# Sparse heads' value products: high and low half of the values in one stationary operand, joined by a permutation product

## The chip, the cores and the metric

One Trainium2 chip, one of its cores. The metric is the device time of one execution in microseconds (us). The cores' engines are named as in the profile: PE is TensorE (matmuls; PEld its weight loads), DVE is VectorE, ACT is ScalarE, POOL is GpSimd, SP issues most of the DMAs.

## What is computed

Two transformer layers on 512 tokens of width 1024. Each layer has eight sliding-window heads (kind "a"), eight sparse heads (kind "b") that share one key and value head and attend to the 128 best keys of an indexer, an output projection with layer norm, then a gated feed-forward part with a second layer norm. The sparse heads' part, cut to what matters here:

```python
_, sel = lax.top_k(idx_score, k_top)
ks = gather(k, sel)
vs = gather(v, sel)
s = jnp.einsum('bqhgd,bqjhd->bqhgj', qb, ks) * (D ** -0.5)
s = jnp.where(valid[:, :, None, None, :], s, NEG)
pr = jax.nn.softmax(s, axis=-1)
o = jnp.einsum('bqhgj,bqjhd->bqhgd', pr, vs)
```

The kernel gathers nothing: it adds a mask of 0 or -1e30 to the scores of all earlier keys, so that `o` is a product of a masked softmax with all values. The heads are 64 wide.

## The kernel before

The tokens stand in four tiles `t` of 128. All matmuls outside the window heads' value products work in the type fp32r, which is coarser than fp32; to keep the accuracy a number is held as a high part (rounded to fp32r) and a low part (the rest), and a product of two such pairs is three matmuls: high by high, high by low, low by high. That is `mm3` (lines 314 to 318).

Attention works in units (kind, `t`, `g`): a group `g` of four heads for one tile of queries, `units` in line 734: first the eight of kind "a", then the eight of kind "b" with `t` rising. `scores` (lines 638 to 673) makes a unit's scores on PE (L656), adds the mask and takes the maximum on DVE (L660), and takes the exponentials and their sums on ACT (L664). `values` (lines 675 to 732) follows two units later. For every block `b` of 128 keys it turns the four heads' probabilities on PE (L698); for kind "b" ACT casts the turned block out of the PSUM bank as the high part (L701) and DVE subtracts to get the low part (L702). Then `pv(b)`, `LAG` = 2 blocks later for kind "b", multiplies with the values. A unit of tile `t` has `t` + 1 blocks, so a layer's eight sparse units have 2 x (1 + 2 + 3 + 4) = 20 blocks.

The result of a unit has to hold two heads on 128 partitions (64 each). So the values stand in a tile `vb[t]` with zeros beside them, the high part in columns 64 to 127 and the low part in 192 to 255 (lines 563 to 576), and `pv` takes for the even head (`u` = 0) a window [values, zeros] and for the odd head [zeros, values]; both add up in the same 256 columns of one bank. With three matmuls for each of the two windows that is six matmuls of 256 columns to a block. At the end of the unit DVE multiplies the bank by the reciprocal sums (L723), ACT casts the product (L730) and POOL takes the low part (L731); they go into `fh` and `fl`, from where the second half of the output projection, `last_o` (lines 820 to 825), reads them.

What sets the order of the instructions: the streams of a layer are Python generators that `Order.run` takes turns with by the costs that they yield; `order.later(delay, fn)` puts off a piece of work until the running cost has grown by `delay` (`tick`). So the program is written with the two halves of the projections, the scores, the values and the top-k mixed. Then the tile framework orders each engine's instructions once more by a simulated timeline. On the chip every engine works its list off in that order. All PSUM tiles come from one pool of eight banks of 512 fp32 columns. While the sparse units run, PE also has the output projection's first half (`rest`, lines 804 to 812, "wsp,slot" in the rows) to do; the second half (`last_o`, 96 matmuls, "wsp,fh") comes when the attention is through, but the scheduler lets it begin under the last unit's products. After `last_o` each tile's sum goes through the first layer norm (`ln_sums`, lines 395 to 404), is turned by PE (`to_features`, lines 406 to 415) and feeds the first `gate_up`.

The weights are split by ACT (L269, high part) and POOL (L270, low part) as soon as one of five buffers `wsp` comes free.

Of the kernel before, what the change touches and what calls it, by code (L numbers as in the profile page):

```python
# [34 lines left out]
NSLOT, NTMP = 28, 12  # L35
D_GI, D_K, D_Q, AHEAD = 9.0, 8.0, 10.0, 2
IDX_PACE, NSTART, R_MAIN, R_TOP = 1.5, 2, 0.75, 0.001
# [4 lines left out]
class Order:  # L42
# [10 lines left out]

    def later(self, delay, fn):
        self.held.append((self.now + delay, fn))

# [31 lines left out]
def hybrid_kernel(ctx: ExitStack, tc: tile.TileContext, x, p, positions, ln_in_g, ln_in_b, w_in,  # L88
# [234 lines left out]
    V.tensor_scalar(idf, jp, 0.0, None, op0=OP.is_equal)  # L323
    V.tensor_copy(idr, idf)
    causal = const.tile([128, S], F32, name="causal")
    G.memset(causal[:, :S - 128], 0.0)
# [184 lines left out]
    for l in range(L):  # L511
# [47 lines left out]
        def kv_out(t, ps):  # L559
# [3 lines left out]
            vb[t] = slot()  # L563
            G.memset(vb[t][:, :320].bitcast(F32), 0.0)
            kss = []
            for c0, n, o in ((0, 2, 0), (2, 1, 256)):
# [3 lines left out]
                for i in range(n):  # L570
                    v = o + (n + i) * 64
                    if c0 + i < 2:
                        A.copy(vt[t][:, 64 + 128 * (c0 + i):128 * (c0 + i + 1)], ps[:, v:v + 64])
                    else:
                        A.copy(vb[t][:, 64:128], ps[:, v:v + 64])
                        V.tensor_tensor(vb[t][:, 192:256], ps[:, v:v + 64], vb[t][:, 64:128], OP.subtract)
                kss.append((c0, n, ks))
# [97 lines left out]
        def values(kind, t, g, st):  # L675

            es, rb, b0, nb = st
            c = g if kind == "a" else 2
            o = acc()[:, :256].rearrange("p (a n) -> p a n", a=2)
            pts = {}  # L680
            lag, cost = LAG[kind], (0.65 if kind == "b" else 0.87)
            if kind == "b":
                yield from wait("x read")

            def pv(b):
                for u in range(2):
                    if kind == "b":
                        h, lo = vb[b0 + b][:, 64 - 64 * u:192 - 64 * u], vb[b0 + b][:, 192 - 64 * u:320 - 64 * u]
                        mm3(o, h, lo, pts[b][0][:, u], pts[b][1][:, u], b == 0 and u == 0, b == nb - 1 and u == 1)
                        continue  # L690
                    f = 64 + 128 * c - 64 * u
                    PE.matmul(o, vt[b0 + b][:, f:f + 128], pts[b][:, u], start=b == 0 and u == 0,  # L692
                              stop=b == nb - 1 and u == 1)
# [26 lines left out]
            for b in range(max(0, nb - lag), nb):  # L720
                pv(b)
                yield cost
            V.tensor_tensor(of, o, rr, OP.mult)  # L723
            if kind == "a":
# [318 lines left out]
```

## Time and profile before

| | before |
|---|---|
| median of 3 runs | 1281.9 us (1280.48 to 1283.91) |
| the profiled execution's own time | 1279.94 us |
| its span, first to last instruction | 1277.8 us |
| PE busy | 1240.9 us, 97% of the span |
| PE weight loads | 1072.5 us, 84% |
| DVE, ACT, POOL busy | 807.2, 569.9, 710.5 us |
| mean granted TensorE clock | 0.988 of full speed |
| DMA | 112.77 MB, mean 88 GB/s |

The busy time of PE counts a matmul from its start to an end that is modelled, and matmuls overlap in the array; so a busy PE is read by the distance from one matmul's start to the next. A row of the timeline gives the start, the duration, the engine and line, the operation with the tiles it writes and reads, and in brackets the idle time before it with what ended that. The wait of an instruction is put down to what came last.

### The profile page before, as it was taken

The numbers are of one execution on the slowest core, as the hardware profiler recorded it, in microseconds if no ns is written. First come the engines' busy times: TensorE is split into PE (matmuls) and PEld (weight loads), VectorE is DVE, ScalarE is ACT, GpSimd is POOL, SyncE is SP. The second block draws the span as 40 slices with busy tenths as digits, with TensorE's granted clock in tenths as the row PEclk, the third lists the DMA queues.
The fourth block names the chain that finished last, engine by engine and source line by source line (L and its number), as shares of the span: only waits on it lengthen the run. The fifth ranks groups of instructions, "written<-read, shape, count | busy, mean of one in ns | idle before, by whom it ended". The sixth has DMA issues, their size and how long they took to land.

```text
span 1277.8 us, 18295 instructions
## 1 busy us (share of the span) xinstructions
PE 1240.9 (97%) x6632; PEld 1072.5 (84%) x6632; DVE 807.2 (63%) x1762; ACT 569.9 (45%) x1192; POOL 710.5 (56%) x589
## 2 busy tenths in 40 slices
PE   6899999899999999999999999999999999999996
PEld 4799889788888888888898998979888888888885
DVE  7799855864545454545679996675736363645376
ACT  2567765344333433334336677743434342434320
POOL 7777532357474757573068855234656575747422
PEclk9899999999999999999998999999999999999998
DMA  5133221333232324134023313104242423231321
GB/s 173 51 98 101 66 68 34 99 115 92 91 112 86 117 81 131 34 100 142 12 68 104 111 34 117 49 20 135 93 133 67 132 74 124 83 99 38 111 83 50
DMA packets 89122, 112.77 MB, mean 88 GB/s; under 512 B 5444, under 2 KB 65860, under 8 KB 89032
## 3 DMA queue, kind: packets, MB, share of 16 engines
q1 hardware_dynamic: 88360, 111.58, 28.2%
q8 instruction: 52, 0.85, 0.3%
q14 instruction: 38, 0.31, 0.1%
q10 hardware_dynamic: 672, 0.03, 0.0%
HBM read 109.49 MB, written 2.10 MB: 87 GB/s over the span
## 4 chain that ended last, share of the span: by engine, by line
PE 83%; DVE 7%; POOL 4%; issue 2%; DMA 2%; ACT 1%; SPq 0%; DVEq 0%; POOLq 0%; ACTq 0%
PE bank L316 25%; PE bank L317 25%; PE bank L318 25%; PE bank L656 3%; PE bank L698 2%; POOL wsp L270 2%; PE bank L692 2%; POOL wsp L248 1%; DMA wst<-in_w_pg_dram 1%; PE bank L486 1%; DVE work L620 1%; DVE x L404 1%; PE bank L412 1%; PE bank L715 1%; DVE fl L415 1%
## 5 line engine op out<-in xcount | busy, mean ns | idle before, releaser
L270 POOL TENSOR_TENSOR wsp<-wst,wsp 128x1024 fp32r<-128x1024 f32 (+2 forms) x148 | 353.3, 2400 | 270.8 <-ACT wsp L269 265.9
L317 PE MATMUL bank<-fl,wsp 128*128 128x512 f32 (+1 forms) x768 | 285.7, 373 | 2.0 <-DVE fl L415 2.0
L316 PE MATMUL bank<-fh,wsp 128*128 128x512 f32 (+1 forms) x768 | 284.2, 373 | 1.0 <-ACT fh L414 1.0
L318 PE MATMUL bank<-fh,wsp 128*128 128x512 f32 (+1 forms) x768 | 283.9, 372 | 0.0
L269 ACT CAST wsp<-wst 128x1024 fp32r<-128x1024 f32 (+2 forms) x148 | 151.2, 1032 | 167.6 <-PE bank L318 115.7
L841 DVE TENSOR_TENSOR t2k<-bank,t2k 128x512 f32<-128x512 f32 x44 | 30.4, 692 | 221.8 <-PE bank L318 221.8
L317 PEld LDWEIGHTS bank<-fl,wsp 128*128 128x128 f32 x768 | 145.5, 189 | 27.5 <-DVE fl L415 2.4
L316 PE MATMUL bank<-wsp,fh 128*128 128x256 f32 (+3 forms) x512 | 165.8, 327 | 0.7 <-ACT fh L414 0.5
L318 PEld LDWEIGHTS bank<-fh,wsp 128*128 128x128 f32 x768 | 145.4, 189 | 25.1
L316 PEld LDWEIGHTS bank<-fh,wsp 128*128 128x128 f32 x768 | 144.2, 189 | 26.3 <-ACT fh L414 1.9
L318 PE MATMUL bank<-wsp,fl 128*128 128x256 f32 (+3 forms) x512 | 164.8, 323 | 1.1 <-DVE fl L415 1.1
L317 PE MATMUL bank<-wsp,fh 128*128 128x256 f32 (+3 forms) x512 | 165.5, 324 | 0.0
L248 POOL TENSOR_TENSOR wsp<-slot,wsp 128x512 fp32r<-128x512 f32 x100 | 141.2, 1438 | 29.5 <-ACT wsp L247 29.5
L316 PE MATMUL bank<-wsp,slot 128*128 128x512 f32 x392 | 153.7, 392 | 0.0
L317 PE MATMUL bank<-wsp,slot 128*128 128x512 f32 x392 | 152.7, 390 | 0.0
L318 PE MATMUL bank<-wsp,slot 128*128 128x512 f32 x392 | 148.5, 389 | 0.0
L773 DVE TENSOR_TENSOR x<-bank,x 128x512 f32<-128x512 f32 x140 | 91.5, 685 | 88.5 <-PE bank L318 88.5
L873 ACT CAST slot<-t2k 128x256 fp32r<-128x256 f32 (+1 forms) x104 | 49.8, 497 | 144.0 <-DVE t2k L841 102.5
L248 POOL TENSOR_TENSOR wsp<-t2k,wsp 128x512 fp32r<-128x512 f32 x40 | 57.5, 1449 | 92.2 <-ACT wsp L247 92.2
L316 PEld LDWEIGHTS bank<-wsp,fh 128*128 128x128 f32 x512 | 98.2, 192 | 7.6 <-ACT fh L414 1.4
L318 PEld LDWEIGHTS bank<-wsp,fl 128*128 128x128 f32 x512 | 98.0, 192 | 6.8 <-DVE fl L415 1.7
L317 PEld LDWEIGHTS bank<-wsp,fh 128*128 128x128 f32 x512 | 98.5, 192 | 5.8 <-POOL wsp L270 0.2
(166 smaller groups left out, 2186.6 us busy)
## 6 DMA issues: line engine op xcount, KB each, us to landing
wst<-in_w_gu_dram SPq DMA_DIRECT2D x88, 512.0 KB, 3.5
slot<-in_w_down_dram SPq DMA_DIRECT2D x80, 256.0 KB, 2.8
wst<-in_w_in_dram SPq DMA_DIRECT2D x16, 512.0 KB, 3.6
wst<-in_w_o_dram SPq DMA_DIRECT2D x16, 512.0 KB, 3.7
wst<-in_w_pg_dram SPq DMA_DIRECT2D x16, 512.0 KB, 4.4
wst<-in_w_in_dram SPq DMA_DIRECT2D x8, 256.0 KB, 2.7
lng<-in_ln_g_dram SPq DMA_DIRECT2D x4, 512.0 KB, 4.9
lnb<-in_ln_b_dram SPq DMA_DIRECT2D x4, 512.0 KB, 6.7
```

What stands on the lines that cost most here:

```text
L248: G.tensor_tensor(w[:, 1, j], src[j], w[:, 0, j], OP.subtract)
L269: A.copy(w[:, 0, :a * n], st[:, :a * n])
L270: G.tensor_tensor(w[:, 1, :a * n], st[:, :a * n], w[:, 0, :a * n], OP.subtract)
L316: PE.matmul(o, sh, mh, start=start, stop=False, skip_group_check=again)
L317: PE.matmul(o, sh, ml, start=False, stop=False, skip_group_check=again)
L318: PE.matmul(o, sl, mh, start=False, stop=stop, skip_group_check=again)
L656: PE.matmul(ps[:, o:o + nn], qT[kind, t, g][:, j * 128:(j + 1) * 128], kT[c, s][:, k0:k0 + nn], start=(s == 0), stop=(s == 1))
L692: PE.matmul(o, vt[b0 + b][:, f:f + 128], pts[b][:, u], start=b == 0 and u == 0, stop=b == nb - 1 and u == 1)
L698: PE.transpose(ps[:, j * 128:(j + 1) * 128], es[j][:, b * 128:(b + 1) * 128], idf)
L773: V.tensor_tensor(xt[t][:, c], ps, xt[t][:, c], OP.add)
L841: V.tensor_tensor(a, ps[1, f], a, OP.mult)
L873: A.copy(h[0], src)
```

## The change

The stationary operand of a sparse product now holds the values' high and low part side by side, so that no column of it is zero. `vb[t]` is [high, low, high] in three times 64 columns; the window from column 0 is [high, low] and the one from column 64 is [low, high]. A block takes two matmuls for each head, with the probabilities' high part and low part: four matmuls of 256 columns where there were six. The two heads go into two halves of the bank, 512 columns instead of 256: in the left half the partitions 0 to 63 hold what the high values gave for the even head, the partitions 64 to 127 what the low values gave, and in the right half it is the other way round for the odd head.

At the unit's end the halves have to be added across the partitions. ACT copies the whole bank into a tile `low` (type fp32r), and `merge`, put off by `D_LOW` = 1.5 and set at the head of the held list, multiplies it by a permutation `swap` that exchanges the upper and the lower 64 partitions, adding into the same bank: one matmul of 512 columns (line 745 of the changed file). After that DVE multiplies by the reciprocal sums in two instructions of 64 partitions, and ACT and POOL store as before (`store`). The zeroing of `vb` on POOL is gone; the high values are cast with a doubled output. The cost that a sparse product yields to the order is 0.48 instead of 0.65. `swap` is made once, on DVE, from the identity.

```diff
-D_GI, D_K, D_Q, AHEAD = 9.0, 8.0, 10.0, 2
+D_GI, D_K, D_Q, D_LOW, AHEAD = 9.0, 8.0, 10.0, 1.5, 2
...
-    def later(self, delay, fn):
-        self.held.append((self.now + delay, fn))
+    def later(self, delay, fn, soon=False):
+
+        self.held.insert(0 if soon else len(self.held), (self.now + delay, fn))
...
+    swap = const.tile([128, 128], F32R, name="swap")
+    V.tensor_copy(swap[:, :64], idf[:, 64:])
+    V.tensor_copy(swap[:, 64:], idf[:, :64])
...
             vb[t] = slot()
-            G.memset(vb[t][:, :320].bitcast(F32), 0.0)
...
-                        A.copy(vb[t][:, 64:128], ps[:, v:v + 64])
-                        V.tensor_tensor(vb[t][:, 192:256], ps[:, v:v + 64], vb[t][:, 64:128], OP.subtract)
+                        top = vb[t][:, :256].rearrange("p (u d) -> p u d", u=2)[:, :, :64]
+                        A.copy(top, ps[:, None, v:v + 64].to_broadcast([128, 2, 64]))
+                        V.tensor_tensor(vb[t][:, 64:128], ps[:, v:v + 64], vb[t][:, :64], OP.subtract)
...
-            o = acc()[:, :256].rearrange("p (a n) -> p a n", a=2)
+            bk = acc()
+            o = bk[:, :256].rearrange("p (a n) -> p a n", a=2)
+            o2 = bk.rearrange("p (u n) -> p u n", u=2)
             pts = {}
-            lag, cost = LAG[kind], (0.65 if kind == "b" else 0.87)
+            lag, cost = LAG[kind], (0.48 if kind == "b" else 0.87)
...
                     if kind == "b":
-                        h, lo = vb[b0 + b][:, 64 - 64 * u:192 - 64 * u], vb[b0 + b][:, 192 - 64 * u:320 - 64 * u]
-                        mm3(o, h, lo, pts[b][0][:, u], pts[b][1][:, u], b == 0 and u == 0, b == nb - 1 and u == 1)
+
+                        for s in range(2):
+                            PE.matmul(o2[:, u], vb[b0 + b][:, 64 * u:64 * u + 128], pts[b][s][:, u],
+                                      start=b == 0 and u == 0 and s == 0, stop=b == nb - 1 and u == 1 and s == 1,
+                                      skip_group_check=True)
                         continue
...
-            V.tensor_tensor(of, o, rr, OP.mult)
+            if kind == "a":
+                V.tensor_tensor(of, o, rr, OP.mult)
+            else:
+                low = t2k(F32R)
+                A.copy(low, bk)
+                yield 0.0
+                order.later(D_LOW, lambda: merge(kind, t, g, bk, low, rr, of), True)
+                return
+            store(kind, t, g, of)
+
+        def merge(kind, t, g, bk, low, rr, of):
+
+            PE.matmul(bk, swap, low, start=False, stop=True, skip_group_check=True)
+            for u in range(2):
+                r = slice(64 * u, 64 * u + 64)
+                V.tensor_tensor(of[r], bk[r, 256 * u:256 * u + 256].rearrange("p (a n) -> p a n", a=2), rr[r], OP.mult)
+            store(kind, t, g, of)
```

The order of the instructions moves too, since the costs and the list have changed. Three places matter to the prediction; each stands alike in both layers.

First, PE at the end of the sparse unit (`t` = 2, `g` = 1) of layer 0. Before, the products of that unit (bank 2718), then the first of the next unit (bank 2807), then a turn of probabilities:

```order
L316 MATMUL bank_2718<-t2k_2763,slot_910 128x256
L317 MATMUL bank_2718<-t2k_2764,slot_910 128x256
L318 MATMUL bank_2718<-t2k_2763,slot_910 128x256
L316 MATMUL bank_2807<-t2k_2813,slot_751 128x256
L698 MATMUL bank_2841<-idf_89,t2k_2623 128x128
```

Now the same place (this unit has bank 2708, the next one bank 2801):

```order
L697 MATMUL bank_2708<-t2k_2753,slot_911 128x256
L697 MATMUL bank_2708<-t2k_2754,slot_911 128x256
L745 MATMUL bank_2708<-t2k_2799,swap_102 128x512
L697 MATMUL bank_2801<-t2k_2807,slot_754 128x256
L708 MATMUL bank_2838<-idf_89,t2k_2639 128x128
```

The permutation product (L745) stands right behind the unit's last product, with nothing between, though the tile it reads, 2799, is ACT's copy of the very bank that this last product writes. It is so at two of a layer's eight sparse units, (2, 1) and (3, 0); at the others more than two other groups of PE's work stand between, at (2, 0) two turns.

Second, ACT around that copy (tile 2799), now:

```order
L669 ACTIVATE t2k_2744,sums_2702<-t2k_2744,ng_2701 128x512
L737 CAST t2k_2799<-bank_2708 128x512
L669 ACTIVATE t2k_2758,sums_2702<-t2k_2758,ng_2701 128x512
L711 CAST t2k_2807<-bank_2802 128x512
L711 CAST t2k_2816<-bank_2811 128x512
```

and before, where the casts of the next unit's blocks (2813 and 2822) wait behind nothing of the unit (2, 1):

```order
L664 ACTIVATE t2k_2754,sums_2712<-t2k_2754,ng_2711 128x512
L718 COPY t2k_2790<-bank_2787 128x256
L701 CAST t2k_2813<-bank_2808 128x512
L664 ACTIVATE t2k_2768,sums_2712<-t2k_2768,ng_2711 128x512
L701 CAST t2k_2822<-bank_2817 128x512
```

The cast that the next unit's first product reads (2813 before, 2807 now) stood ahead of the last exponential, and now stands behind it and behind the new copy. At the unit (3, 0) the next unit's cast stands directly behind the copy.

Third, ACT at the layer's end, where the layer norms of the tiles 0 to 3 (`x0` to `x3`) meet the splitting of the next weights. Before:

```order
L401 ACTIVATE t2k_3027,lnvar_3025<-x1_86,lnm_3024 128x512
L401 ACTIVATE t2k_3029,lnvar_3025<-x1_86,lnm_3024 128x512
L401 ACTIVATE t2k_3077,lnvar_3075<-x2_87,lnm_3074 128x512
L401 ACTIVATE t2k_3079,lnvar_3075<-x2_87,lnm_3074 128x512
L269 CAST wsp_3102<-wst_2430 128x1024
```

and now:

```order
L406 ACTIVATE t2k_3018,lnvar_3016<-x1_86,lnm_3015 128x512
L406 ACTIVATE t2k_3020,lnvar_3016<-x1_86,lnm_3015 128x512
L270 CAST wsp_3093<-wst_2433 128x1024
L406 ACTIVATE t2k_3068,lnvar_3066<-x2_87,lnm_3065 128x512
L406 ACTIVATE t2k_3070,lnvar_3066<-x2_87,lnm_3065 128x512
```

The first split of new weights stood behind the sums of tile 2 and now stands ahead of them. (Lines of the changed file are 1 to 28 higher than those before: 316 is 317, 401 is 406, 660 is 665, 664 is 669, 698 is 708, 701 is 711.)

## Rows read from the trace of the kernel before

**Rows 1.** The page: share of engines on the chain that ended last.

```profile
PE 83%; DVE 7%; POOL 4%; issue 2%; DMA 2%; ACT 1%; SPq 0%; DVEq 0%; POOLq 0%; ACTq 0%
```

**Rows 2.** Busy time by engine, sparse units of both layers, and 55 to 60 us.

```profile
155.00:218.00 63.00, 62.95 (x408) 56.66 (x407) 36.43 (x102) 40.32 (x104) 20.22 (x23) 1.00 0.21 66
780.00:840.00 60.00, 60.00 (x386) 54.14 (x385) 35.04 (x92) 36.38 (x89) 18.50 (x19) 1.00 0.16 50
...
55.00:60.00 5.00, 4.06 (x21) 3.52 (x20) 4.51 (x12) 4.89 (x14) 1.39 (x4) 0.58 0.02 5
```

**Rows 3.** Groups by line and shape: a third of the sparse products; POOL's zeroing; DVE's scaling.

```profile
L316 PE MATMUL bank<-t2k,slot 128*128 128x256 f32 x80 | 23.2, 290 | 0.0
...
L564 POOL MEMSET slot<- 128x320 f32 x8 | 2.9, 361 | 0.0
...
L723 DVE TENSOR_TENSOR t2k<-bank,t2k 128x256 f32<-128x256 f32 x32 | 13.4, 418 | 13.4 <-PE bank L318 12.4 <-PE bank L692 0.9
```

**Rows 4.** Timeline of PE: ends of 21 projection matmuls and 12 sparse products; a first projection matmul.

```profile
177.64 0.39 PE L316 MATMUL bank<-wsp,slot 128*128 128x512 f32 x1
...
182.17 0.39 PE L318 MATMUL bank<-wsp,slot 128*128 128x512 f32 x1
182.40 0.28 PE L316 MATMUL bank<-t2k,slot 128*128 128x256 f32 x1
...
183.71 0.28 PE L318 MATMUL bank<-t2k,slot 128*128 128x256 f32 x1
183.83 0.52 PE L656 MATMUL bank<-slot 128*128 128x384 f32 x2
...
185.77 0.38 PE L715 MATMUL bank<-idf,rb 128*128 128x128 f32 x2
185.91 0.48 PE L316 MATMUL bank<-wsp,slot 128*128 128x512 f32 x1
186.22 0.39 PE L317 MATMUL bank<-wsp,slot 128*128 128x512 f32 x1
```

**Rows 5.** Timeline of ACT and PE: from PE to ACT and from ACT to PE.

```profile
211.29 0.60 PE L698 MATMUL bank<-idf,t2k 128*128 128x128 f32 x4
211.93 0.59 ACT L701 CAST t2k<-bank 128x512 fp32r<-128x512 f32 x1 [0.69 <-PE bank L698]
...
255.62 1.08 ACT L414 CAST fh<-bank 128x512 fp32r<-128x512 f32 x2 [5.55 <-PE bank L412]
256.25 1.20 PE L316 MATMUL bank<-fh,wsp 128*128 128x256 f32 x6 [0.24 <-ACT fh L414]
```

**Rows 6.** Timeline of ACT: a cast of 512 columns, an exponential, the next cast.

```profile
202.08 0.59 ACT L701 CAST t2k<-bank 128x512 fp32r<-128x512 f32 x1
202.56 0.72 ACT L664 ACTIVATE t2k<-t2k,ng 128x512 f32<-128x512 f32 x1
...
203.28 0.57 ACT L701 CAST t2k<-bank 128x512 fp32r<-128x512 f32 x1
```

**Rows 7.** Timeline of ACT, POOL, DVE and PE at the end of layer 0.

```profile
233.77 2.93 ACT L269 CAST wsp<-wst 128x1024 fp32r<-128x1024 f32 x3
234.88 12.28 POOL L270 TENSOR_TENSOR wsp<-wst,wsp 128x1024 fp32r<-128x1024 f32 x4 [15.91 <-ACT wsp L269]
234.02 0.69 DVE L770 CUSTOM_DVE_ANT_0 x<-bank,x 128x512 f32<-128x512 f32 x1 [0.47 <-PE bank L318]
234.63 1.28 DVE L402 SCALAR_TENSOR_TENSOR x<-x,lnm,lng 128x1024 f32<-128x1024 f32 x1
236.08 3.16 DVE L404 SCALAR_TENSOR_TENSOR x<-x,lns,lnb 128x1024 f32<-128x1024 f32 x1
239.29 1.10 PE L412 MATMUL bank<-idf,x 128*128 128x128 f32 x8 [1.71 <-DVE lns L353]
248.29 1.09 PE L412 MATMUL bank<-idf,x 128*128 128x128 f32 x8 [0.41 <-DVE x L404]
261.30 2.40 POOL L270 TENSOR_TENSOR wsp<-wst,wsp 128x1024 fp32r<-128x1024 f32 x1 [14.15 <-ACT wsp L269]
```

**Rows 8.** Timeline of PE at the end of layer 1: 14 matmuls from 861.46 to 864.61.

```profile
858.63 1.09 PE L412 MATMUL bank<-idf,x 128*128 128x128 f32 x8 [1.72 <-DVE lns L353]
...
861.46 0.58 PE L317 MATMUL bank<-fl,wsp 128*128 128x256 f32 x1 [0.99 <-DVE fl L415]
...
864.61 0.33 PE L317 MATMUL bank<-fl,wsp 128*128 128x256 f32 x1
864.78 0.28 PE L318 MATMUL bank<-fh,wsp 128*128 128x256 f32 x1
```

**Rows 9.** Timeline of DVE at the start of the kernel.

```profile
6.35 1.41 DVE L368 BATCH_NORM_STATS2 bst<-x 128x6 f32<-128x512 f32 x2 [4.39 <-DMA x<-in_x_dram]
```

More of the change, by code (lines that the diff above doesn't have):

```diff
@@ L722, in values, with store @@
                 yield cost
-            V.tensor_tensor(of, o, rr, OP.mult)
+            if kind == "a":
[13 more added lines that the diff above has]
+            store(kind, t, g, of)
+        def store(kind, t, g, of):
             if kind == "a":
```

## The prediction, made before the changed kernel ran

> **What bounds the kernel now.** First I read the chain of waits on the page: PE holds 83% of it, DVE 7%, POOL 4%, ACT 1% [rows 1]. So PE's list, worked off in order, sets the time, and a change counts by what it takes from that list and by the waits it puts in. Second I read the table of stretches for the place where the change acts. From 155 to 218 us, the sparse units of layer 0, PE is busy 62.95 of 63 us at the full granted clock, and from 780 to 840, those of layer 1, 60.00 of 60; ACT has 40.32 and DVE 36.43 of the 63, POOL 20.22 [rows 2]. There is no idle PE time there for a new operation to hide in, nor any in which a removed one was hidden already. Third I read the groups and the timeline for the prices. A modelled end makes a matmul look longer than it holds up the next (a sparse product shows 290 ns [rows 3]), so I count from start to start.
>
> **What is removed and added on PE.** The two layers have 2 x 20 blocks, and a block loses two of its six products: 80 products of 256 columns, as many as line 316 alone shows [rows 3]. Twelve of them stand from 182.40 to 183.83: 1.43/12 = 0.119 us each [rows 4]. Removed: 80 x 0.119 = 9.5 us. Added is one product of 512 columns at the end of each unit, 16 in all. The nearest row is a run of 21 projection matmuls of 512 columns, 177.64 to 182.40: 4.76/21 = 0.227 us each [rows 4]; 16 x 0.227 = 3.6 us. PE gains 5.9 us by this count. From below the added price is that of these rows. From above I take 0.31, what the first projection matmul behind another kind of matmul takes, 185.91 to 186.22 [rows 4], which would make 5.0 and a gain of 4.5. I take 5.9, since the permutation product mostly stands between other products.
>
> These distances show that a 512-column matmul costs a little under two of 256 columns. The Trainium skill (TensorE: Matmul & The Clock Gate, section Back-to-back issue gap) gives the warm distance as columns over 2.4 GHz plus 2.5 ns. By it the two prices would be about 109 and 216 ns and the gain 8.7 - 3.5 = 5.3 us, an estimate from that page; the rows lie some 5 to 9% above it, and the sum goes by the rows.
>
> **The new waits inside the sparse units.** A permutation product reads ACT's copy of the bank that the unit's last product has just written. At two of a layer's eight units, (2, 1) and (3, 0), the order has nothing between the two on PE. With the last product's start as 0 its end is at 0.28 [rows 4]. ACT begins 0.04 after PE's end [rows 5] and needs some 0.58 for 512 columns from a bank [rows 5, 6], to 0.90; PE starts 0.04 after ACT's end (a cast of 0.59 from 255.62, PE at 256.25 [rows 5]), at 0.94. PE was free at 0.12. That is a wait of 0.82 at each of four units, 3.3 us, and no work of PE's can be moved into it, since the list is in order.
>
> What queues behind counts too. At (2, 1) ACT has, behind the copy, an exponential (0.72) and only then the cast (0.58) that the next unit's first product reads; before, that cast stood ahead of the exponential. From start to start ACT needs 0.48 behind a cast and 0.72 behind an exponential [rows 6]; so the cast starts at 0.32 + 0.48 + 0.72 = 1.52 and ends at 2.10, and PE could start at 2.14; it comes free at 0.94 + 0.23 = 1.17. Wait: 0.97. At (3, 0) the cast follows the copy directly: start 0.80, end 1.38, PE at 1.42 against 1.17, wait 0.25. At (2, 0) two turns of probabilities cover the copy, but the next product again waits for a cast behind it, 0.25. So a layer loses 2 x 0.82 + 0.97 + 0.25 + 0.25 = 3.1, both layers 6.2 us. The lower end is 3.3, the four direct waits with everything behind them covered. The upper end I set at 8: a unit's bank now stays taken until copy, permutation product and two DVE operations are done, and all PSUM tiles share eight banks, so one or two turns may wait for a bank as well (about 0.9 each, a copy and the better part of a scaling).
>
> **The end of a layer.** In the order ACT's first split of new weights moves ahead of tile 2's sums. What it releases is POOL's first L270. POOL and DVE hinder each other there: from 234.88 POOL takes 12.28 us for four of these instructions, where one alone takes 2.40 [rows 7]; DVE's L402, begun at 234.63 before POOL, takes 1.28, and L404, begun at 236.08 under it, takes 3.16 [rows 7]. The Trainium skill (SBUF — State Buffer, section Who interferes with whom) says that a DVE instruction with two SBUF inputs and a GpSimd instruction shut each other out for a whole instruction, and whichever starts first goes first. These rows agree, and by that page the order in which the two begin is what matters, which speaks against this change.
>
> In the new order POOL's first split can start 0.65 us or more earlier, ahead of tile 2's L402 (now L407). So one more DVE operation on the way from the sums to PE's turns falls under a POOL instruction. Blocked once costs 3.16 - 1.28 = 1.9 us, not blocked costs 0; I take 1.6, close to the upper end, because the pair collides already in rows 7 and only POOL's earlier start (it is done sooner too) gives something back. PE waits for this DVE chain, 1.71 us at 239.29 and 0.41 at 248.29 [rows 7]. In layer 0 I take the second, 0.4, as swallowed by the first. So +1.2 and +1.6 = +2.8 us, with the ends 0 and 3.8.
>
> **At nothing.** POOL's eight memsets of 361 ns [rows 3] go, but POOL was busy only 1.39 of 5 us there [rows 2]. The making of `swap` falls in DVE's idle 4.39 us at the start [rows 9]. The high values' cast writes twice the columns in a stretch where PE is no bound for it (PE 4.06 of 5 [rows 2]); even 0.06 each for eight would be 0.5. ACT's 16 copies (16 x 0.58 = 9.3 us) and DVE's 16 more scalings (at most 16 x 0.418 = 6.7 [rows 3]) fit into the room of rows 2 by their sum; what they cost by their place in the queue is counted above. SP issues its transfers in the old order. If DVE's cover goes, the scaling only delays `last_o`, whose first 42 matmuls stand ahead of the last unit's merge.
>
> **The sum.** -5.9 + 6.2 + 2.8 = +3.1 us. The profiled execution took 1279.94 (span 1277.8 and 2.1 around it), so 1283.0 by its own account; the median of the runs is 1281.9, 2.0 higher, and the prediction is 1285.0. About 0.3%, 3.8 us, is what a measurement of this kernel can tell from no change; "the same" is therefore 1278.1 to 1285.7.
>
> **The rivals.**
> - The gain goes through but for the direct waits: -5.9 + 3.3 - 0.4 = -3.0, so 1278.9, and down to 1276.0 if ACT's copies too find cover. For it: ACT is free a third of these stretches [rows 2], so the casts behind the copies may be done in time, and layer ends may fall out as before. Against it: the order has the cast behind copy and exponential, where it was ahead. Chance 0.28, about half of it beyond the bound of "faster".
> - Waits as above, but the layer's end loses nothing, since DVE's operation begins before POOL's or POOL is simply done sooner: -5.9 + 6.2 = +0.3, so 1282.2. Chance 0.20.
> - The longer idle stretches of PE let its granted clock fall, a loss on top. At the end of layer 1, after waits of 1.72 and 0.99 us, 14 matmuls from 861.46 take 3.15 us, 0.22 each, about the lower level of 1.2 GHz, where 14 x 0.119 would be 1.7 [rows 8]: 1.5 us lost. At the end of layer 0 six matmuls from 256.25 take 1.20 us in all [rows 5], less than six at that distance, so the clock was not down throughout. With a wait there 1.2 us longer it would fall too: +1.5, and as much again if layer 1 stays down longer. 1285.0 + 1.5 to 3.0 = 1286.5 to 1288.0. It decides from the point where PE's waits at layer 0's end reach those of layer 1. Against it: the forecast's waits are a microsecond each and PE is full before. Chance 0.20.
> - That the change does not do what it says: excluded, since the order has 160 sparse products for 240, and 16 permutation products.
>
> **How the numbers follow.** My forecast has 0.32; most of it (0.22) lies inside the bound. Faster: 0.15, half of the first rival. Slower: 0.20 from the clock and 0.10 of the forecast, 0.30. The rest, 0.13 + 0.20 + 0.22, is 0.55 for the same. The range runs from 1277.0, which leaves out the better part of "all copies covered", to 1288.0, the clock's upper end.
>
> **What would show it.** Right: 160 rows of the sparse product and 16 of the permutation product with 0.23 from start to start; in each layer two idle times of PE of 0.8 ended by ACT's copy, at (2, 1) and (3, 0), and one of about 1.0 ended by ACT's cast; at both layer ends a scaling of DVE of 3 us under a POOL split, and PE's wait before the turns of tile 1 over a microsecond longer. Wrong: idle times of PE in the sparse stretch that sum to under 3 us in a layer (the first rival), DVE's operations at the layer end with their old lengths (the second), or a granted clock below full at the end of layer 0 (the third). A PE busy time that falls by other than 5.9 at full clock would refute the count itself.

## The result and the profile after

The changed kernel takes 1290.64 us (median of 4 runs, 1289.58 to 1291.60) against 1281.19 (4 runs, 1279.59 to 1283.91) for the kernel before: a ratio of 1.0069, 95% interval 1.0056 to 1.0081, some 9 us slower. The profiled execution has a span of 1289.7 us, 11.9 more than the one before. Forecast were 1285.0, within 1277.0 to 1288.0: the kernel got slower, as the forecast's sum had it, but by three times as much, and outside the range.

The page's shares of the chain answer to [rows 1]; PE still sets the time:

```profile
PE 83%; DVE 7%; POOL 3%; issue 2%; ACT 2%; DMA 2%; SPq 0%; DVEq 0%; POOLq 0%; ACTq 0%
```

The table of stretches says more (as in [rows 2]: stretch, its length, busy time and instructions of PE, weight loads, DVE, ACT and POOL, granted clock, DMA share, GB/s). The sparse units of both layers:

```profile
157.00:220.00 63.00, 60.54 (x362) 52.03 (x363) 38.80 (x109) 43.89 (x114) 21.05 (x25) 1.00 0.22 70
784.00:845.00 61.00, 58.82 (x352) 50.58 (x351) 39.74 (x112) 42.24 (x110) 19.94 (x23) 1.00 0.20 62
```

PE was busy in all of it before and now idles 2.5 and 2.2 us, even by the modelled ends; ACT and DVE have more to do. The groups by line and shape that answer to [rows 3]:

```profile
L697 PE MATMUL bank<-t2k,slot 128*128 128x256 f32 x160 | 29.3, 295 | 1.5 <-ACT t2k L711 1.4
...
L697 PEld LDWEIGHTS bank<-t2k,slot 128*128 128x128 f32 x160 | 23.7, 189 | 6.0 <-ACT t2k L711 3.2 <-DVE t2k L712 0.9
...
L748 DVE TENSOR_TENSOR t2k<-bank,t2k 64x256 f32<-64x256 f32 x32 | 13.4, 418 | 2.9 <-PE bank L745 2.7
...
L737 ACT CAST t2k<-bank 128x512 fp32r<-128x512 f32 x16 | 9.3, 582 | 22.2 <-PE bank L697 22.2
L745 PE MATMUL bank<-t2k,swap 128*128 128x512 f32 x16 | 7.1, 443 | 2.8 <-ACT t2k L737 2.8
```

160 products, 16 copies of 582 ns, 16 permutation products, as forecast. PE's timeline at the units (2, 1) and (3, 0) of layer 0, and ACT's at (2, 1), show the join (the last product, ACT's copy of the bank and the permutation product behind it):

```profile
207.90 1.01 PE L697 MATMUL bank<-t2k,slot 128*128 128x256 f32 x4
209.64 0.49 PE L745 MATMUL bank<-t2k,swap 128*128 128x512 f32 x1 [0.73 <-ACT t2k L737]
210.83 0.39 PE L697 MATMUL bank<-t2k,slot 128*128 128x256 f32 x1 [0.69 <-ACT t2k L711]
...
213.42 1.56 PE L697 MATMUL bank<-t2k,slot 128*128 128x256 f32 x11
215.65 0.49 PE L745 MATMUL bank<-t2k,swap 128*128 128x512 f32 x1 [0.68 <-ACT t2k L737]
216.14 0.39 PE L697 MATMUL bank<-t2k,slot 128*128 128x256 f32 x1
...
209.00 0.59 ACT L737 CAST t2k<-bank 128x512 fp32r<-128x512 f32 x1 [0.17 <-PE bank L697]
209.49 0.72 ACT L669 ACTIVATE t2k<-t2k,ng 128x512 f32<-128x512 f32 x1
...
210.20 1.06 ACT L711 CAST t2k<-bank 128x512 fp32r<-128x512 f32 x2
```

The bracket counts from a modelled end, so the wait is read from start to start: from 209.64 to 210.83 are 1.19 us where 0.23 would do, 0.96 lost. ACT was free when the last product ended (0.17 idle before its copy), so the wait ahead of 209.64 is the way from PE to ACT and back; the one behind it is ACT's queue, where an exponential stands between the copy and the cast that the next product reads. Four products that take 1.01 (from 207.90), where 0.72 would do, hide a further wait of some 0.3 that no bracket names.

The timeline of POOL, DVE and PE at the end of layer 0 answers to [rows 7]:

```profile
238.14 2.41 POOL L271 TENSOR_TENSOR wsp<-wst,wsp 128x1024 fp32r<-128x1024 f32 x1 [6.97 <-ACT wsp L270]
239.52 2.11 DVE L407 SCALAR_TENSOR_TENSOR x<-x,lnm,lng 128x1024 f32<-128x1024 f32 x1
...
241.68 3.24 DVE L409 SCALAR_TENSOR_TENSOR x<-x,lns,lnb 128x1024 f32<-128x1024 f32 x1
245.06 1.06 PE L417 MATMUL bank<-idf,x 128*128 128x128 f32 x8 [3.13 <-DVE x L409]
```

POOL now begins ahead of DVE's L407, which takes 2.11 where the old L402 took 1.28; L409 follows under the next split with 3.24, and PE waits 3.13 us.

To see where 11.9 us lie, the span is cut at PE's turns of x (L412 before, L417 now), which every kernel here has in the same order: those of the last tile before a layer's attention part (projections, top-k and all units) and those of the tiles 0 to 2 behind it. Two more executions, one of each kernel, were profiled later (their runs stand below) and are set beside the first two:

| stretch, us | before | changed | before, 2nd | changed, 2nd |
|---|---|---|---|---|
| start to layer 0's attention | 32.65 | 34.02 | 31.83 | 31.78 |
| attention, layer 0, to the turns of tile 0 | 203.89 | 206.87 | 205.08 | 208.04 |
| turns of tile 0 to those of tile 1 | 2.75 | 4.17 | 2.75 | 4.17 |
| turns of tile 1 to those of tile 2 | 9.00 | 10.53 | 10.81 | 9.68 |
| to layer 1's attention | 411.55 | 411.40 | 411.64 | 411.53 |
| attention, layer 1 | 196.04 | 198.58 | 196.72 | 199.67 |
| turns of tile 0 to tile 1 | 2.75 | 4.17 | 2.75 | 4.17 |
| turns of tile 1 to tile 2 | 9.88 | 10.51 | 9.00 | 9.50 |
| to the end | 409.33 | 409.44 | 409.33 | 409.09 |

What repeats is the attention (mean of the pairs +3.0 and +2.7) and the turns of tile 0 to tile 1 (+1.42 each). That the two pairs give the same +3.0 in layer 0 is chance: from the first sparse product to the turns of tile 0 layer 0 takes 66.50 in both executions of the kernel before, and 68.01 and 69.58 in the changed one (layer 1: 66.46 and 66.48, then 67.98 and 69.63); the rest of the 3.0 lies ahead of the first sparse product, where 137.39 and 138.58 stand against 138.87 and 138.46. The start and the turns of tile 1 to 2 differ within one kernel as much as between the two.

Inside the attention, PE's distances from start to start, summed by kind of matmul, give for layer 0 before and now: sparse products 14.96 and 12.71, permutation products 0 and 3.40, turns of probabilities (the window heads' included) 12.39 and 12.97; together 27.35 and 29.08. Layer 1 gives 27.32 and 29.09. These sums (below "the sparse sum") are what the experiments are compared by. Some 0.3 of the 0.58 by which the turns rose is bookkeeping and no time: the last turn ahead of a projection or score product counts 0.03, and that product, which is not in the sum, 0.08 more than usual; there are 18 such turns in the new order and 22 in the old. The plain stretch from the first sparse product to the turns of tile 0 grew by 1.5 in each layer (66.50 to 68.01, 66.46 to 67.98), the sum by 1.7.

### The profile page after: what moved, and what is told of

It is laid out like the page before. It is cut to its first block, busy times and chain, and to the rows that moved or that the text cites. A ratio compares the mean times of both kernels' runs of the same rounds, so it can differ in the third digit from the quotient of the medians.

```text
span 1289.7 us, 18216 instructions
## 1 busy us (share of the span) xinstructions
PE 1244.3 (96%) x6568; PEld 1070.7 (83%) x6568; DVE 815.1 (63%) x1780; ACT 576.7 (45%) x1208; POOL 707.4 (55%) x581
## 4 chain that ended last, share of the span: by engine, by line
PE 83%; DVE 7%; POOL 3%; issue 2%; ACT 2%; DMA 2%; SPq 0%; DVEq 0%; POOLq 0%; ACTq 0%
PE bank L317 24%; PE bank L318 24%; PE bank L319 24%; PE bank L661 3%; PE bank L708 2%; PE bank L702 2%; PE bank L697 2%; POOL wsp L271 1%; POOL wsp L249 1%; DMA wst<-in_w_pg_dram 1%; PE bank L491 1%; DVE x L409 1%; PE bank L725 1%; PE bank L417 0%; DVE fl L420 0%
## 5 line engine op out<-in xcount | busy, mean ns | idle before, releaser
L317 PEld LDWEIGHTS bank<-fh,wsp 128*128 128x128 f32 x768 | 146.1, 192 | 26.6 <-ACT fh L419 1.9
L319 PEld LDWEIGHTS bank<-fh,wsp 128*128 128x128 f32 x768 | 147.0, 191 | 24.8
L317 PEld LDWEIGHTS bank<-wsp,fh 128*128 128x128 f32 x512 | 99.7, 195 | 8.3 <-DVE work L625 1.4
L318 PEld LDWEIGHTS bank<-wsp,fh 128*128 128x128 f32 x512 | 99.9, 195 | 5.7 <-POOL wsp L271 0.3
```

What stands on the lines that cost most here:

```text
L317: PE.matmul(o, sh, mh, start=start, stop=False, skip_group_check=again)
L318: PE.matmul(o, sh, ml, start=False, stop=False, skip_group_check=again)
L319: PE.matmul(o, sl, mh, start=False, stop=stop, skip_group_check=again)
```

## Experiments

Theories: **W**, PE waits at the join because the copy and the next casts share ACT's queue; **E**, at the layer's end POOL's split blocks DVE's layer norm; **O**, the moved order elsewhere costs time. Ratios are to the kernel before, run beside each.

**1. The last unit as before.** The unit (3, 1) uses six products and a zeroed window again, which POOL fills beside the packed values.

```diff
+OLD = [(3, 1)]
...
+            G.memset(vb[t][:, 192:].bitcast(F32), 0.0)
...
+                        G.tensor_copy(vb[t][:, 256:320], vb[t][:, :64])
+                        G.tensor_copy(vb[t][:, 384:448], vb[t][:, 64:128])
...
+                    if kind == "b" and (t, g) in OLD:
+                        h, lo = vb[b0 + b][:, 256 - 64 * u:384 - 64 * u], vb[b0 + b][:, 384 - 64 * u:512 - 64 * u]
+                        mm3(o, h, lo, pts[b][0][:, u], pts[b][1][:, u], b == 0 and u == 0, b == nb - 1 and u == 1)
+                        continue
...
-            if kind == "a":
+            if kind == "a" or (t, g) in OLD:
```

> The last sparse unit of a layer, (3, 1), is computed as before (six products to a block into 256 columns, a zeroed window, no copy and no permutation product); the other seven units stay packed. In the order of ACT the first split of new weights then stands behind tile 2's sums again. Theory E (the layer end is lost because POOL's split starts ahead of tile 2's L407, so that L407 and L409 fall under POOL; the longer PE wait then lets the granted clock fall): the layer ends come back to their old length, 16.96 and 17.78 us from PE's turns of tile 1 to the next stage, and PE's wait for L409 from 3.13 to about 1.7; that gives 1.4 + 1.5 us in layer 0 and 1.4 + 0.6 in layer 1, 4.9 in all. The unit itself costs 8 products of 0.12 more and one permutation product of 0.24 less in a layer, 1.4 in all. Net -3.5: about 1287. Rival (the order there is harmless, the loss comes from the later end of the attention part): +1.4, about 1292, and the PE wait stays near 3 us.

Measured 1288.56, ratio 1.0053 (1.0039 to 1.0067). PE's wait for tile 1 fell to 1.70, tile 0 to tile 1 to 2.74 in both layers; DVE's layer norm operation there began 0.25 us before POOL (236.16, 236.41) and took 1.28. That is as E says. But the turns of tile 1 to tile 2 took 9.94 and 11.02, so what the expectation had put down to the clock was not given back.

**2. No join.** Copy, permutation product and `merge` are left out; DVE's two scalings at a unit's end stay.

```diff
-                low = t2k(F32R)
-                A.copy(low, bk)
...
-            PE.matmul(bk, swap, low, start=False, stop=True, skip_group_check=True)
...
```

> Left out: what the low values give (the copy of the bank, the permutation product and its adding); the products stay packed, four to a block. Theory W (the packing itself gains what was counted, about 9.1 us, and the join takes it back by PE's waits, 4.0 us a layer, by 16 products of 0.24, and by the layer's end, 4.9): about 16 us less than the changed kernel, 1274 to 1276, and no PE idle time of over 0.3 us between the sparse products. Rival (the packed products or the moved order are slow by themselves): 1281 or more, with the sparse products spaced well over 0.125 us.

Measured 1276.21, ratio 0.9957 (0.9944 to 0.9969). The join costs 14.4 us in all, with what it does to the layer's end (tile 0 to tile 1 takes 2.74 again in both layers). The sparse sum is 23.69 and 23.99, 3.7 and 3.3 us under the kernel before; the stretch from the first sparse product to the turns of tile 0 is 62.63 and 62.94, 3.9 and 3.5 less; 40 products of 0.119 would be 4.8. The products stand 0.135 apart (10.77/80). The group of their weight loads shows why:

```profile
L697 PEld LDWEIGHTS bank<-t2k,slot 128*128 128x128 f32 x160 | 23.7, 189 | 3.2 <-DVE t2k L712 1.1
```

They stand idle for 3.2 us; the only wait that the row names is 1.1 us for DVE's low part of a turned block (L712); the three groups of the kernel before had 0.3, 0.6 and 0.4, and the changed kernel has 6.0. So even without a join the packing is worth 7.0 to 7.4 us of PE's time, not 9.5; the measured time fell by 5.7. The reading is that PE, with fewer products, catches up with the engines that prepare the blocks; the experiment keeps DVE's additional scalings, so it does not tell these two apart.

**3. DVE makes the copy.**

```diff
-                A.copy(low, bk)
+                V.tensor_copy(low, bk)
```

> The copy of the bank is made by DVE instead of ACT; all else is as changed. In the order the permutation products of (2, 1) and (3, 0) then have other work between them and the unit's last product. Theory W (PE waits because ACT, the engine of the copy, has the next unit's casts in the same queue): the four waits of about 0.9 and those of 0.96 and 0.26 behind them go, 3 to 4 us a layer; the layer's end stays as in the changed kernel: about 1290.6 - 7 = 1283.6. Rival (at the tail of the sparse units PE is starved whatever engine copies, since DVE has the low parts' subtractions in its own queue): 1289 to 1292, with waits for DVE in the place of those for ACT.

Measured 1293.14, slower still: 1.0093 (1.0079 to 1.0107). The four waits at the join are gone, as W expects: the sparse sum is 27.36 in layer 0 and 27.37 in layer 1, 1.7 less than with ACT's copy, two waits in a layer being left, 0.72 for an ACT cast and 0.66 for POOL behind one permutation product. But the order moved as well, and other work now stands ahead of the permutation products, so the run does not separate ACT's queue from the place in PE's list. What was won there was lost at the layer's end: 4.18 from tile 0 to 1 and 13.39 and 14.25 from tile 1 to 2. In the table of stretches PE's granted clock is at the lower level there, 0.50:

```profile
240.50:250.80 10.30, 5.97 (x25) 5.31 (x26) 9.98 (x23) 3.42 (x7) 5.08 (x2) 0.50 0.64 201
```

DVE is busy 9.98 of 10.30 us, and PE's two longest waits there are for DVE (3.14 and 2.57): its queue has become the bound.

**4. The old cost.**

```diff
-            lag, cost = LAG[kind], (0.48 if kind == "b" else 0.87)
+            lag, cost = LAG[kind], (0.65 if kind == "b" else 0.87)
```

> Only the cost that a sparse product yields to the order is put back from 0.48 to 0.65. Theory O (some 2 us of the loss come from the moved order at the start of the top-k stage, where PE waits for DVE's work and the granted clock is low): about 1288.6, with the stretch from the first layer turn to the sparse units shorter by about a microsecond in each layer. Rival (the cost decides nothing there, the stretch is longer through the phase of the clock or through DVE's work): 1290 to 1291.

Measured 1290.18, ratio 1.0069 (1.0057 to 1.0082). No gain, and the stretch from the last turns of x to the first sparse product is no shorter (139.30 and 130.62 for 138.87 and 130.60): O falls as far as this cost sets the order.

**5. ACT's split behind tile 2's sums again.**

```diff
+            if "sq" in quarter:
+                with tc.issue_after(quarter.pop("sq")):
+                    A.copy(w[:, 0, :a * n], st[:, :a * n])
...
+            sq = A.activation(t2k(), xt[t][:, h * 512:(h + 1) * 512], AF.Square, bias=nm, accum_out=var[:, h:h + 1])
+        if key[0] == "1" and t == 2:
+            quarter["sq"] = sq.ins
```

`sq` is the last of the squares in tile 2's sums.

> The changed kernel with one thing put back: at the end of each attention part ACT's first split of new weights stands behind the sums of tile 2 again (what follows it on ACT and DVE comes as before; PE, POOL and SP keep their order but for a few rows). Theory E: PE's wait for tile 1 falls from 3.13 to about 1.7 us in both layers, 2.8 in all, and the granted clock stays low for a shorter time, 0 to 2 us more: 1286 to 1288. Rival (the wait comes from the last unit's later end, not from the split): 1290 to 1291, with L407 and L409 of tile 1 as long as in the changed kernel.

Measured 1290.15, ratio 1.0073 (1.0060 to 1.0085): no gain, a miss. ACT's order was as before, but PE's wait grew to 4.15. The timeline of POOL and DVE:

```profile
238.74 2.39 POOL L275 TENSOR_TENSOR wsp<-wst,wsp 128x1024 fp32r<-128x1024 f32 x1 [7.99 <-ACT wsp L272]
...
238.74 3.48 DVE L413 SCALAR_TENSOR_TENSOR x<-x,lnm,lng 128x1024 f32<-128x1024 f32 x1
...
242.50 3.00 DVE L415 SCALAR_TENSOR_TENSOR x<-x,lns,lnb 128x1024 f32<-128x1024 f32 x1
```

Both begin at 238.74 (in layer 1 at 861.59), and DVE (L413 is L407 of the changed kernel) takes 3.48, 2.20 more than alone. In the kernel before DVE was first by 0.25 us [rows 7]. ACT's cast stood where it had stood before the change and the loss stayed; the runs differ in which of the two begins first.

**6. Both repairs.** The edits of 3 and 5.

> Both repairs together: the bank is copied by DVE and the first split stands behind tile 2's sums. If the two losses add up, the sparse units' PE time is that of the kernel before (27.4 us a layer for products, permutation products and turns, as in the run with DVE's copy) and the layer ends are those of the kernel before with 0 to 1 us for the clock in each: 1281.9 to 1284. Rival (DVE's copies and scalings push its layer norms back, as at tile 3 in the run with DVE's copy): 1287 or more.

Measured 1287.24, ratio 1.0045 (1.0033 to 1.0057). The sparse sum is 27.36 and 27.51, tile 0 to 1 takes 2.95, but tile 1 to 2 takes 11.10 and 12.24. The rival was right: DVE's layer norms are late.

**7. Three units unpacked**, `OLD = [(2, 1), (3, 0), (3, 1)]` in the edit of 1.

> The units (2, 1), (3, 0) and (3, 1) are computed as before, the five others stay packed; these five have work between their last product and the permutation product. Theory W (the join costs little where PE has other work to cover it): a layer saves 18 products of 0.12 = 2.2 us and pays 5 x 0.24 + 0.26 = 1.5 for permutation products and the waiting cast behind one, the layer end is the old one: 1280 to 1282.5, level with the kernel before. Rival (a join costs about the mean of 14.4/16 = 0.9 us wherever it stands): 10 x 0.9 - 4.3 = +4.7, about 1286.5.

Measured 1285.31, ratio 1.0026 (1.0016 to 1.0036), nearer to the rival. Yet a join is cheap where it is covered: the five permutation products of a layer take 1.51 (expected 1.5). The products fell only from 14.96 to 13.44 (expected -2.2), and from the first sparse product to the turns of tile 0 a layer takes 66.73 and 66.82, 0.2 and 0.4 more than before, where 0.7 less was expected. It is the packing that gains less than counted. That leaves some 3 us of the 3.9 which the traces do not assign.

**8. Before, with the permutation's tile made and unused.**

```diff
+    swap = const.tile([128, 128], F32R, name="swap")
+    V.tensor_copy(swap[:, :64], idf[:, 64:])
+    V.tensor_copy(swap[:, 64:], idf[:, :64])
```

> The kernel before with only the tile of the permutation made and not used. A control: what the start and the clock do without the change. If the 1.35 us that the changed kernel's profile shows at the start (18.5 to 33.6 us) come from the making of the tile, the stretch is about 15.2 here too; if they are a matter of when the granted clock falls, it is 11 to 15 and the time 1281 to 1283. The sparse units and both layer ends are to be as in the kernel before within the clock's share, 0 to 1.5 us for a layer end.

Measured 1281.53, ratio 0.9999 (0.9990 to 1.0009). The tile costs nothing that this shows; the start takes 31.88.

**9. and 10. Both kernels once more**, for their traces.

> The kernel before once more, for its trace alone. If the 1.35 us at the start and the clock's part of the layer ends are a matter of the moment at which the granted clock falls, the start (to the first three tiles' turns) lies anywhere from 31.8 to 34.0 us and the stretch behind PE's turns of tile 1 anywhere from 9.0 to 10.9, with the order unchanged. Rival (they belong to the kernel): 32.6 and 9.0 to 9.9 again.

> The changed kernel once more, for its trace alone. The start lies anywhere from 31.8 to 34.0 us if it is the moment of the clock's fall that sets it; the products, permutation products and turns of the sparse units take 29.1 us a layer again, and PE's wait for tile 1 is 3.13 again, since these are set by the order.

The spans are 1279.9 and 1287.6, the stretches those of the table. The sparse sum before is 27.35 and 27.32 again; in the changed kernel it is 30.66 and 30.50, not the 29.1 expected. The stretches around the join of (2, 1) in layer 0 say why:

```profile
200.00:206.00 6.00, 5.93 (x41) 4.97 (x39) 5.20 (x12) 5.36 (x14) 3.48 (x3) 1.00 0.30 93
206.00:209.00 3.00, 1.58 (x11) 1.06 (x10) 1.60 (x6) 2.83 (x9) 0.29 (x1) 1.00 0.55 172
209.00:212.40 3.40, 3.40 (x19) 3.40 (x17) 2.09 (x4) 1.25 (x3) 0.80 (x2) 0.50 0.00 0
```

PE is busy 1.58 of 3.00 us while it waits at the join, and then the granted clock is 0.50 for 3.4 us. This fall, which only some executions of the changed kernel have, costs 1.6 us in each layer (69.58 and 69.63 from the first sparse product to the turns of tile 0, for 68.01 and 67.98 without it). The profiled execution of experiment 11 has it in layer 0 alone (69.65 and 67.97).

**11. and 12. POOL's first split waits for DVE**, in both kernels. DVE writes one column of the split's output behind tile 1's last layer norm operation, so that POOL cannot begin before.

```diff
+            if "gate" in quarter:
+                with tc.issue_after(quarter.pop("gate")):
+                    V.memset(w[:, 1, :1].bitcast(F32), 0.0)
             G.tensor_tensor(w[:, 1, :a * n], st[:, :a * n], w[:, 0, :a * n], OP.subtract)
...
+        end = V.scalar_tensor_tensor(xt[t], xt[t], rs, b_t, op0=OP.mult, op1=OP.add)
+        if key[0] == "1" and t == 1:
+            quarter["gate"] = end.ins
```

> The changed kernel, and POOL's first split of new weights at each layer end waits for a one-column write of DVE that stands behind tile 1's L409 in DVE's order. Theory E, mended (which of POOL's split and DVE's layer norm begins first decides, not where ACT's cast stands): tile 2's L407 and tile 1's L409 take 1.28 us each in place of 2.11 and 3.24, the PE wait for tile 1 falls from 3.13 to about 0.4, 2.7 us in each layer, and the granted clock falls less: 1282.5 to 1285.5. Rival (POOL's later split makes PE wait for new weights, or other DVE work is blocked in their place): 1288 or more.

> The kernel before with the same gate and nothing else. Theory E: tile 1's L404 takes 1.28 us in place of 3.16, PE's wait for tile 1 falls from 1.71 to near 0 in each layer: 2 x 1.7 = 3.4 us less and up to a microsecond more where the granted clock no longer falls: 1276.5 to 1278.5, faster than both kernels. Rival (the next weights come later by the same time, PE waits there): 1281 to 1283.

Measured 1287.39, ratio 1.0040 (1.0026 to 1.0054), and 1281.33, ratio 0.9994 (0.9985 to 1.0003). The gate held one split only, and POOL's order put another weight ahead of it. In the changed kernel L407 was freed (1.28), L409 not (3.26), tile 0 to 1 took 3.35; in the kernel before L404 still took 3.21. So the theory was not yet tried.

**13. and 14. All three splits gated**, the edit of 11 with `[end.ins] * 3` (each split takes one entry).

> As the gated version of the changed kernel, but all three splits of new weights at a layer end wait for DVE (one column each, behind tile 1's L409); with one gated, POOL took another weight first. Theory E, mended: L407 and L409 both take 1.28 us, PE's wait for tile 1 falls from 2.3 to about 0.3, 2 us a layer less than with one gate: 1282 to 1285. Rival (POOL's later splits make PE wait for weights, or block the layer norm of the next tile in place): 1287 or more.

> The same three gates in the kernel before. Theory E: L404 of tile 1 takes 1.28 in place of 3.2, PE's wait for tile 1 falls from 1.7 to near 0: 1277 to 1279.5, faster than both kernels. Rival (as above, the block moves to the next tile's layer norm or PE waits for weights): 1281 to 1283.

The changed kernel: 1281.72, ratio 1.0002 (0.9993 to 1.0011), 8.9 us less than ungated. The kernel before: 1277.95, ratio 0.9967 (0.9955 to 0.9978), faster than both. The timeline of DVE, PE and POOL in the gated changed kernel (L410 and L412 are L407 and L409, L422 is L417):

```profile
237.75 1.28 DVE L410 SCALAR_TENSOR_TENSOR x<-x,lnm,lng 128x1024 f32<-128x1024 f32 x1
239.08 1.27 DVE L412 SCALAR_TENSOR_TENSOR x<-x,lns,lnb 128x1024 f32<-128x1024 f32 x1
...
240.50 1.06 PE L422 MATMUL bank<-idf,x 128*128 128x128 f32 x8 [0.33 <-DVE wsp L273]
240.51 11.40 POOL L274 TENSOR_TENSOR wsp<-wst,wsp 128x1024 fp32r<-128x1024 f32 x4 [11.10 <-DVE wsp L273]
```

POOL begins behind both operations, which have their length alone. PE waits 0.33 instead of 3.13, tile 0 to 1 takes 1.37 and tile 1 to 2 9.23 in both layers. PE waits for no weights; the next tile's norms now fall under POOL (2.35 and 2.14), and PE waits 0.87 for them. In the gated kernel before, PE's timeline has the turns of both tiles on end:

```profile
237.93 1.97 PE L417 MATMUL bank<-idf,x 128*128 128x128 f32 x16
```

and in its table of stretches the clock stays at its upper level:

```profile
238.00:248.00 10.00, 8.18 (x65) 7.45 (x63) 10.00 (x26) 4.60 (x10) 9.10 (x4) 1.00 0.35 107
```

Theory E is shown. The two gated kernels differ by 3.8 us. In the traces this is 1.5 in each layer from the first sparse product to the turns of tile 0 (67.97 and 67.95 against 66.50 and 66.47) and 0.5 in each from tile 0 to tile 1 (1.37 against 0.87).

**15. DVE's copy and all splits gated**, the edits of 3 and 13.

> The change with both of its losses mended: DVE copies the bank and all three splits are gated. The sparse units then take PE 27.4 us a layer as in the kernel before and the layer end is that of the gated kernel before, 0 to 1 us longer since DVE's queue is fuller: 1277 to 1281. Rival (the tail of the attention part delays DVE so that the layer norm, not POOL, sets the layer end): 1284 or more.

Measured 1285.92, ratio 1.0037 (1.0024 to 1.0050): the rival. The sparse sum is 27.36 and 27.53, and L407 and L409 are free, but DVE took a sum of another tile between them (L409's start 2.25 us behind L407's, 1.33 in 13), so PE waited 1.27, and tile 1 to 2 took 11.53 and 11.31. The repairs do not add up: both lean on DVE, and PE's longest waits there, 1.27 and 1.83, are for DVE.

## Why the prediction was wrong

**PE's own gain: size nearly right.** Forecast -9.5 + 3.6 = -5.9. Without the waits the products fell by 14.96 - 10.42 = 4.5 in a layer, 9.1 in all; permutation products stand 0.24 from their followers where nothing waits, 3.8 in all. Net -5.3. The page's busy time of PE, 1244.3 for 1240.9, can't test this count, since it holds modelled ends and the stretches at the lower clock.

**The waits at the join: right in size.** Forecast 3.1 a layer: 0.82, 0.97, 0.82, 0.25, 0.25. Start to start less the normal distance: 0.89, 0.96, 0.84, 0.26, 0.26, together 3.2. The unit with two turns between, which the forecast calls (2, 0), is (1, 1): its permutation product stands at 192.01, behind the 24th sparse product of the layer, and its wait is as forecast; at (2, 0) (204.22) nothing waits. The first and the third of them are the way from PE to ACT and back with nothing between on PE, the others ACT's queue, as the rows at 209.00 to 210.20 show for (2, 1).

**The step that failed** is "ACT's 16 copies ... and DVE's 16 more scalings ... fit into the room of rows 2 by their sum; what they cost by their place in the queue is counted above". It was not all counted: only the casts behind ACT's copies were, and DVE's queue was put at nothing. In the unit (2, 1) PE waits three times more, about 0.3, 0.2 and 0.3, together 0.8 us a layer and 1.6 in all that the sum lacked. DVE is busy 4.55 of the 4.60 us from 204.24 to 208.84, and two of the three waits are for its low parts (L712). One of them, DVE and PE's weight load:

```profile
205.46 0.85 DVE L748 TENSOR_TENSOR t2k<-bank,t2k 64x256 f32<-64x256 f32 x2
206.34 0.69 DVE L712 TENSOR_TENSOR t2k<-bank,t2k 128x512 fp32r<-128x512 f32 x1
...
207.08 0.41 PEld L697 LDWEIGHTS bank<-t2k,slot 128*128 128x128 f32 x3 [0.24 <-DVE t2k L712]
```

ACT had cast this block by 205.53; DVE begins its low part at 206.34, behind the two scalings of 0.85 that were one of 0.42, so the additional one alone is more than the 0.24 that PE waits. The third wait no row names. Experiment 2, where no join is left, gives 7.0 to 7.4 us of the 9.5 and so points the same way. From the first sparse product to the turns of tile 0 the time thus grew by 1.5 a layer, 3.0 in all, in place of the +0.3 of the forecast (-5.9 + 6.2): 0.6 by the smaller net gain, 0.2 by the join, 1.6 by these waits, the rest unassigned.

**The clock was placed as a rival and at one spot only.** The forecast had it fall at the end of layer 0, for 1.5 to 3.0 us. It falls there in the first profile (tile 1 to 2 takes 10.53 for 9.00), but in the second look at the kernel before it falls there too (10.81), so this fall is not shown to be the change's. The two rows, the changed kernel and the second look at the one before:

```profile
246.20:253.00 6.80, 6.18 (x27) 5.88 (x28) 6.62 (x18) 2.95 (x7) 3.33 (x2) 0.50 0.67 198
```

```profile
241.00:248.00 7.00, 6.25 (x28) 5.95 (x29) 7.00 (x16) 2.77 (x6) 6.49 (x3) 0.51 0.59 179
```

The fall that was seen with the change alone is the one behind the join, up to 3.2 us for both layers, and no rival named it.

**The layer's end: right in size, by its own steps.** Forecast +2.8, one more operation of DVE under a POOL split; measured 2 x 1.42 = 2.84 from tile 0 to tile 1, L407 at 2.11 and L409 at 3.24. Where the forecast put the cause in ACT's order, experiment 5 refutes it: with that order back PE's wait grew, to 4.15. The start times count, and they lie tenths of a microsecond apart. The Trainium skill (SBUF — State Buffer, section Who interferes with whom) has the order in which the two begin decide which of them holds the other off. The traces agree: in experiment 1 DVE begins 0.25 us before POOL and takes 1.28; in the changed kernel POOL begins 1.38 before DVE, whose operation ends 1.08 behind POOL's (241.63 and 240.55).

**The sum.** 3.0 (sparse units) + 2.8 (layer ends) + 0 to 3.2 (the clock behind the join) = 5.8 to 9.0, against some 9 measured and 3.1 forecast. The first profile has no fall behind the join and is the longer of the two, so the clock there does not make up the difference in every execution. What of the rest is chance in the moment of the clock's falls at start and layer ends, and what is not, stays open: the spans of the two pairs differ by 11.9 and 7.7.

## What to carry to other kernels

Work taken off the bounding engine is worth its full time only until the engines that feed it become late (here 7.0 to 7.4 us of 9.5), so look at the feeders' queue in the very stretch, not at their share over 60 us. A step that leaves the array, is copied by a busy engine and comes back puts that engine's whole queue on the path; it needs independent work of the array between. Where two engines exclude each other, hold back the one that nobody waits for: a one-column write as a gate gave 3.8 us in the kernel before, about as much as the change could have won by an estimate with no wait at the join left (7.0 to 7.4 of experiment 2 less 3.8 for the permutation products, 3.2 to 3.6).

## What was not expected of the hardware

- POOL and DVE beginning at the same moment (238.74 and, in layer 1, 861.59, within 4 ns): DVE lost both times, by 2.20 us.
- About a microsecond of waiting, twice in 3 us in a stretch where PE is otherwise full, was followed by 3.4 us at the lower clock level in one execution and by none in another of the same kernel (sparse sums 30.66 and 29.08). What decides between the two is open.
- With the order unchanged, the start of the same program takes 31.8 to 34.0 us and a layer's end 9.0 or 10.8, by when the granted clock falls.
